# Two-layer streaming encoder in float32 precision: a fused multiply-add for three right operands of layer 1, and four changes of order in the attention part

## The chip, the cores and the metric

The kernel runs on one core of a Trainium2 chip. Its time is the device time of the whole program in microseconds (us), taken as the median over several executions. The engines of the core are TensorE (PE, matrix products), VectorE (DVE), ScalarE (ACT), GpSimd (POOL) and SyncE (SP), on whose queue all transfers between device memory and the on-chip SBUF are issued. Each engine works its instructions off in order and waits on semaphores for the others. Matrix products land in PSUM banks, from which an instruction of DVE or ACT takes them (an eviction).

## The reference

The input `x` has 2048 rows of 1024 floats. Layer 1 is a gated mixer, layer 2 a banded attention; both add to the residual stream, and a norm ends the whole:

```python
h = rms_norm(x, a_norm_g)
u, v, z = split(h @ w_in, 3)              # 1024 x 6144
v = layer_norm(gelu(v), ln_g, ln_b)
y = gelu(u) * (w_s_masked @ v + b_s) * silu(z)   # in groups of 128 rows
x = x + y @ w_out                          # 2048 x 1024
k, v = split(rms_norm(x, g_kv) @ w_kv, 2)
q, z = split(rms_norm(x, b_norm_g) @ w_qz, 2)
o = softmax(q k^T / 8 + rel_bias, over 9 chunks of 64) v     # 16 heads of 64
x = x + (o * silu(z)) @ wb_out
return rms_norm(x, final_norm_g)
```

## The kernel before

**Precision.** Every float32 operand is split into a high part `hi` (rounded to the matmul's format) and the remainder `lo`; a product is three matmuls, `hi*hi`, `hi*lo` and `lo*hi` (lines 118 to 120, so that one product is told by three lines). The split is an ACT copy and a DVE subtraction (line 446).

**Layer 1.** `h @ w_in` is cut into six column blocks `n = 0..5` (two for v, four for u and z), and `y @ w_out` is block `"o"`. Each block is a 2x2-block Strassen-Winograd product: seven products ("phases" 1 to 7, in the order 1, 2, 6, 5, 7, 4, 3) of a left operand S, made of row blocks of x, and a right operand T, made of the weights' quarters `rw_<phase>_<row><column><q>`. A phase has eight steps j, one 512-column product P of twelve matmuls each, in one of four PSUM banks (tag "mm"). `evict` (line 600 and about) adds P into the tiles x, y, c and d, with the row factor `rs` of the norm on some of them.

The norm's gain `ga` belongs to the weights' rows. Before the change, `make_t` applied it so: in phases 1, 2 and 3 together with the split (`fused`: ACT writes `hi = w*ga`, DVE `lo = w*ga - hi` in one scalar_tensor_tensor, line 527); in phases 7, 4 and 6 by ACT multiplications in place (line 494, for block 0 of phase 6 by DVE, line 492), after which POOL made the Winograd sums (`comb`, line 454), half by half: phase 6 `t1 = b12 - b11`, kept in a tile `ch`, then `b22 - t1*ga`; phase 7 `b22 - b12`; phase 4 `b21 - (the result of phase 6)`. Phase 5 takes `t1*ga` as it is and splits it whole (1024 columns).

**What sets the order.** Layer 1's work is laid out by steps: `add_t` puts the load, the sum (`combine`) and the split (`finish`) of each right operand at offsets in steps before the phase that uses it (`offs`); `at` and `put` do this for the scaling of x (`x_scale`), the layer norm of v (`va`, `vl`, lines 878 to 888), the mixing and the stores. The tile scheduler then orders each engine's instructions; dependencies without a semaphore (`behind`, `in_order`, `on_beat`, `paced_by_pj`) pin one instruction behind another on an engine. The raw weights of a block have four buffers ("raw"), so each later load waits until an earlier one has been used up.

In block 0, x itself is scaled by its row factors while the products run: `x_scale(blk, half)` multiplies half of a row block (`ha`, `hb`) by the factors `rbc` (line 794), the first half at step j + 3, the second at j + 22.

**Attention.** It goes over four stretches t of 512 rows and, in each, over eight pairs p of heads. A pair has eight units u (two heads by four blocks of 128 rows): scores s (line 1495), softmax (lines 1503 to 1514, the last being POOL's scaling of `pr`), transposes tp (1530), their split into pt (1534, 1535), and `value`, the product pv (1555), drained by `drain` (1574, 1575) through a tile `ot`. Into the gaps between them `ahead` feeds other matmuls by `take`: the projections pj of the next pair's q, k and z (`project` and `gate`, weights `raw_b`, line 253) and the output projection of the previous stretch (`outs`), `SHARE[t][p]` steps of it per pair. The last stretch's own output products come after its last pair; their left operand's sums are made in `last_open` and `last_sums` on POOL, before and between the units of the last pair. The first q of a pair are copied from one half of the partitions to the other by a transfer (line 1425) before a score can use them.

Of the kernel before, what the change touches and what calls it, by code (L numbers as in the profile page):

```python
# [9 lines left out]
F32 = mybir.dt.float32  # L10
# [23 lines left out]
def trunk_kernel(  # L34
# [57 lines left out]
    ga = cst.tile([P, KD], F32, name="ga")  # L92
    kg = cst.tile([P, KD, 1], F32, name="kg")
# [152 lines left out]
    def weights(t, p, c):  # L246
        name = f"b{t}_{p}_{c}"
        raw = raw_w(t, f"raw_{name}")
        w = w_tile(f"wh_{name}"), w_tile(f"wl_{name}")
        if t or p < 2:  # L250
            nc.sync.dma_start(raw[:], wk3[p][c][:])
        else:
            nc.sync.dma_start(raw[:], w_kqz[p, :, c, :])
# [138 lines left out]
    with ExitStack() as actx:  # L392
# [64 lines left out]
        def make_t(n, ph, src, nq, where, chain_of):  # L457
# [10 lines left out]
            fused = n != "o" and ph in (1, 2, 3)  # L468
# [14 lines left out]
            def combine(q):  # L483
# [3 lines left out]
                def gain(t, r, dve=False):  # L487
                    for i in range(2) if n != "o" and not fused else ():
                        t_ = t[:, i * 512 : i * 512 + 512]
                        k = r * 4 + q * 2 + i  # L490
                        if dve:
                            nc.vector.tensor_scalar(t_, t_, ga[:, k : k + 1], None, op0=mul)
                        else:
                            nc.scalar.mul(t_, t_, ga[:, k : k + 1])
                    return t

# [5 lines left out]
                elif ph == 7:  # L502
                    v = raw(1, 1)
                    comb(v, v, raw(0, 1))
                elif ph == 4:
                    v = chain[n](q)
                    comb(v, raw(1, 0), v)
                elif ph == 5:
                    v = chain[n](2 + q)
                else:  # L510
                    if q == 0:
                        chain[n] = chain_of()
                    b22 = raw(1, 1)
                    t1 = comb(chain[n](2 + q), rows.pop((0, 1, q)), rows.pop((0, 0, q)))
                    v = comb(chain[n](q), b22, gain(t1, 0, n == 0))
                vs[q] = v

            def finish(q):
                out[q] = where(q)
                if fused:  # L520
                    for i in range(2):
                        c_ = slice(i * 512, i * 512 + 512)
                        k = need[0][0] * 4 + 2 * q + i
# [267 lines left out]
        def x_scale(blk, half):  # L791
            h = (hb if blk % 2 else ha)[blk // 2]
            h_ = h[:, half * 512 : half * 512 + 512].rearrange("p (k c) -> p k c", k=4)
            nc.vector.tensor_tensor(
                h_, h_, rbc[:, blk].broadcast_to([P, 4, P]), op=mul
            )

# [175 lines left out]
        for n in range(6):  # L973
            for ph in PH:
                where = in_t(n, ph)
                s = start.get((n, ph), start[0, ph])
                if n == 0 or (n == 1 and ph in (1, 2)):
                    offs = ((-6, 1), (-5, 1), (-3 if (n, ph) == (0, 6) else -4, 1))
# [16 lines left out]
        at(-LOOK, lambda: (x_load(0), nc.sync.dma_start(ga[:], a_norm_g)))  # L995
# [3 lines left out]
        for j in range(NJ):  # L999
# [8 lines left out]
            put(j + 22, x_scale, 2 * j, 1)  # L1008
# [367 lines left out]
    with ExitStack() as bctx:  # L1376
# [103 lines left out]
        def score(t, p, u):  # L1480
# [33 lines left out]
            nc.gpsimd.tensor_scalar(  # L1514
                pr[:, c0:], pr[:, c0:], sl, 1.0, op0=ALU.mult, op1=ALU.mult
            )
# [50 lines left out]
        def drain(t, p, hd, po):  # L1567
# [5 lines left out]
            ot = sb.tile([P, T], F32, tag="ot", name=f"ot{t}_{h}", bufs=1)  # L1573
# [79 lines left out]
        def last_open():  # L1653
# [10 lines left out]
            def third():  # L1664
                for cs in (slice(0, 512), slice(512, 1024)):
                    on_beat(tg(la["s3"][:, cs], la["00"][:, cs], la["10"][:, cs], op=sub))
# [7 lines left out]
        def last_sums(cs):  # L1674
            x_ = {n: a[:, cs] for n, a in la.items()}
            return [
                lambda a=a, b=b, c=c, op=op: on_beat(tg(x_[a], x_[b], x_[c], op=op))
# [233 lines left out]
        def o_all(t):  # L1911
# [4 lines left out]
            (0,) * 8, (0, 0, 0, 0, 13, 13, 22, 8), (7, 7, 7, 7, 7, 7, 14, 0), (6, 6, 6, 6, 6, 7, 7, 12)  # L1916
# [66 lines left out]
        for u in range(2):  # L1983
            take(first, 4)
# [109 lines left out]
```

## Time and profile before

| | us |
|---|---|
| median of three runs (lowest, highest) | 2630.78 (2628.39, 2632.53) |
| profiled execution | 2632.79 |
| its span | 2631.0 |
| PE busy in it | 2582.2 |
| DVE, ACT, POOL busy | 1926.8, 1412.9, 904.4 |

The span runs from the first to the last instruction of the profiled execution. An engine's busy time leaves out waiting. A view by stretches gives each engine's busy time between two moments of the span, the clock that TensorE was granted (1.00 is full) and the share of the time in which the transfer engines were busy. A view of waits gives for each instruction group how long it stood idle and what ended that.

### The profile page before, as it was taken

The page shows a single profiled execution, that of the slowest core. Times are in us where ns is not written, and L with a number is a line of the kernel's source. Part 1 is how long each engine was busy: PE and PEld are TensorE (multiplying, and loading weights), DVE is VectorE, ACT ScalarE, POOL GpSimd, SP SyncE. Part 2 cuts the span into 40 slices and gives each one's busy share as a digit, 9 for nine tenths or more (in the row PEclk, how much of TensorE's full clock was granted, in tenths as well). Part 3 has the DMA queues.
Part 4 walks back from the last instruction along what each step waited for, and adds up shares of the span by engine and source line. Part 5 has one row for each costly group of instructions (what it writes and reads, how often), then busy time and mean ns, then how long its engine had stood idle before and what let it go on. Part 6 is the DMA issues. An engine that isn't in the chain of part 4 may idle for free.

```text
span 2631.0 us, 37991 instructions
## 1 busy us (share of the span) xinstructions
PE 2582.2 (98%) x12752; PEld 2156.3 (82%) x12752; DVE 1926.8 (73%) x3050; ACT 1412.9 (54%) x2521; POOL 904.4 (34%) x875
## 2 busy tenths in 40 slices
PE   9999999999999999999999999999999999999997
PEld 7788788888888888888788878888887888888886
DVE  5984796876768667767857767778777777877677
ACT  7553373553544535443345556666656655666564
POOL 3812245163251323204134234344342322332245
PEclk9999999999999999999999999999999999999999
DMA  8899978989899879878887677778787666775666
GB/s 314 288 351 341 363 278 320 344 303 358 316 338 328 304 262 330 318 243 297 293 305 252 204 237 231 231 247 266 237 277 260 220 208 221 250 228 163 193 226 253
DMA packets 281346, 723.46 MB, mean 275 GB/s; under 512 B 29760, under 2 KB 69696, under 8 KB 281152
## 3 DMA queue, kind: packets, MB, share of 16 engines
q1 hardware_dynamic: 281152, 721.03, 78.8%
q8 instruction: 102, 1.67, 0.3%
q14 instruction: 92, 0.75, 0.1%
HBM read 528.50 MB, written 181.93 MB: 270 GB/s over the span
## 4 chain that ended last, share of the span: by engine, by line
PE 81%; DMA 6%; DVE 6%; ACT 2%; issue 2%; POOL 1%; SPq 0%; DVEq 0%; POOLq 0%; ACTq 0%
PE P L118 9%; PE P L120 9%; PE P L119 9%; PE pj L118 6%; PE pj L120 6%; PE pj L119 6%; PE pv L1555 5%; PE s L1495 4%; PE tp L1530 4%; PE Po L120 4%; PE Po L119 4%; PE Po L118 4%; PE vp L120 2%; PE vp L119 2%; PE vp L118 2%
## 5 line engine op out<-in xcount | busy, mean ns | idle before, releaser
L118 PE MATMUL P<-T,S 128*128 128x512 f32 x1248 | 494.8, 396 | 13.7 <-DVE x L602 5.1
L120 PE MATMUL P<-T,S 128*128 128x512 f32 x1248 | 488.3, 391 | 0.0
L119 PE MATMUL P<-T,S 128*128 128x512 f32 x1248 | 487.9, 391 | 0.3 <-DVE T L527 0.3
L1514 POOL TENSOR_SCALAR pr<-pr,ns 128x640 f32<-128x640 f32 (+4 forms) x256 | 208.6, 815 | 529.6 <-DVE ns L1513 448.4
L118 PE MATMUL pj<-hh_b,wh_b 128*128 128x512 f32 x768 | 319.4, 416 | 0.2 <-ACT wh_b L235 0.2
L120 PE MATMUL pj<-hh_b,wl_b 128*128 128x512 f32 x768 | 303.9, 396 | 0.9 <-DVE wl_b L236 0.9
L119 PE MATMUL pj<-hl_b,wh_b 128*128 128x512 f32 x768 | 302.8, 394 | 0.1
L1510 ACT ACTIVATE pr<-pr,ns 128x640 f32<-128x640 f32 (+4 forms) x256 | 195.5, 764 | 191.9 <-DVE ns L1503 191.0
L118 PEld LDWEIGHTS P<-T,S 128*128 128x128 f32 x1248 | 235.2, 188 | 63.3 <-DVE x L602 3.6
L120 PEld LDWEIGHTS P<-T,S 128*128 128x128 f32 x1248 | 235.0, 188 | 50.9 <-DVE S L446 0.4
L119 PEld LDWEIGHTS P<-T,S 128*128 128x128 f32 x1248 | 235.4, 189 | 45.3 <-DVE T L527 0.6
L1535 DVE TENSOR_TENSOR pt<-tp,pt 128x640 fp32r<-128x640 f32 (+4 forms) x256 | 188.4, 736 | 44.5 <-ACT pt L1534 41.8
L1503 DVE CUSTOM_DVE_ANT_0 pr<-s,bias 128x640 f32<-128x640 f32 (+4 forms) x256 | 188.0, 734 | 36.5 <-PE s L1495 30.8
L1534 ACT CAST pt<-tp 128x640 fp32r<-128x640 f32 (+4 forms) x256 | 158.9, 621 | 52.9 <-PE tp L1530 48.1
L1530 PE MATMUL tp<-ident,pr 128*128 128x128 f32 x1120 | 166.6, 275 | 10.9 <-DVE pt L1535 10.2
L120 PEld LDWEIGHTS pj<-hh_b,wl_b 128*128 128x128 f32 x768 | 144.5, 188 | 35.2 <-DVE wl_b L236 2.9
L1530 PEld LDWEIGHTS tp<-ident,pr 128*128 128x128 f32 x1120 | 130.4, 141 | 46.6 <-issue 16.9
L118 PEld LDWEIGHTS pj<-hh_b,wh_b 128*128 128x128 f32 x768 | 145.3, 189 | 18.2 <-ACT wh_b L235 1.9
L119 PEld LDWEIGHTS pj<-hl_b,wh_b 128*128 128x128 f32 x768 | 145.5, 189 | 16.8 <-DVE hl_b L193 0.6
L1555 PEld LDWEIGHTS pv<-pt,V 128*128 128x128 f32 x896 | 143.2, 188 | 18.5 <-DVE pt L1535 2.6
L1555 PE MATMUL pv<-pt,V 128*128 128x256 f32 (+3 forms) x896 | 153.8, 319 | 0.4 <-DVE pt L1535 0.4
L236 DVE TENSOR_TENSOR wl_b<-raw_b,wh_b 128x1024 fp32r<-128x1024 f32 x96 | 120.7, 1259 | 25.9 <-ACT wh_b L235 25.0
(308 smaller groups left out, 5852.0 us busy)
## 6 DMA issues: line engine op xcount, KB each, us to landing
S<-hsd SPq DMA_DIRECT2D x224, 512.0 KB, 5.9
rw<-in_w_a SPq DMA_DIRECT2D x108, 512.0 KB, 6.4
raw_b<-wk SPq DMA_DIRECT2D x78, 512.0 KB, 4.2
A<-ytd SPq DMA_DIRECT2D x72, 512.0 KB, 6.3
hsd<-S SPq DMA_DIRECT2D x56, 512.0 KB, 5.8
V<-vhd SPq DMA_DIRECT2D x56, 512.0 KB, 5.5
bias<-reld SPq DMA_DIRECT2D x64, 320.0 KB, 4.0
va<-vd SPq DMA_DIRECT2D x32, 512.0 KB, 5.9
```

What stands on the lines that cost most here:

```text
L118: first = mm(ps, lh, rh, start=first, stop=False)
L119: mm(ps, lh, rl, start=False, stop=False)
L120: mm(ps, ll, rh, start=False, stop=last)
L236: tv(wl[:], raw[:], wh[:].bitcast(F32), op=sub)
L1495: mm(ps[:, sg, :w], q[:, qb * P : (qb + 1) * P], kx[:, koff + sg * w : koff + (sg + 1) * w], start=i == 0, stop=i == 1,)
L1503: nc.vector.tensor_tensor_reduce(out=pr[:, c0:].rearrange("p (a b) -> p a b", a=nseg), in0=ps[:, :nseg, :w], in1=bias[:, c0:].rearrange("p ...
L1510: nc.scalar.activation(pr[:, c0:], pr[:, c0:], AF.Exp, scale=-1.0, bias=nm, accum_out=sl)
L1514: nc.gpsimd.tensor_scalar(pr[:, c0:], pr[:, c0:], sl, 1.0, op0=ALU.mult, op1=ALU.mult)
L1530: ins = tpose(tp[:, b, :], pr[:, b * P : (b + 1) * P], ident[:])
L1534: nc.scalar.copy(oh, tp[:, b0:5, :].rearrange("p a b -> p (a b)"))
L1535: nc.vector.tensor_tensor(pt[:, 2560 + o + b0 * P : 2560 + o + 640], tp[:, b0:5, :].rearrange("p a b -> p (a b)"), oh.bitcast(F32), op=ALU ...
L1555: mm(po[:, q0 * P : q1 * P], vtl[t, p][:, i, hs], rhs, start=(i == blocks[0] and j == 0), stop=(i == 7 and j == 1),)
```

## The change

It has these parts.

1. Right operands of phases 6, 7 and 4 of all six blocks: no ACT gain on the weights that are subtracted, and no POOL subtraction. DVE does both in one `scalar_tensor_tensor` per half (`times`): `b22 + t1*(-ga)`, `b22 + b12*(-ga)`, `b21*ga - v`. The gain of `b22` remains on ACT. POOL keeps `t1 = b12 - b11`. A constant `nga = -ga` is made once. Phase 5 joins the fused phases: its gain and split go together, half by half.
2. Block 0: phase 6's loads, sums and splits stand at steps -7, -6 and -3 (before: -6, -5, -3); the second half of an even block's `x_scale` moves from j + 22 to j + 32 and is pinned behind the latest eviction.
3. Attention, start: the load of the raw weights of pair 3, part 1, is ordered behind the projection matmul eight places back (`paced_by_pj(ins, 8)`), and the first `take` before the first score is 6 then 2, instead of 4 and 4.
4. Attention, end: `SHARE` of the last stretch; POOL's sums of the last pair (`third`, `last_sums`) are pinned behind the latest softmax scaling (`on_ease`) instead of, or besides, the latest transposes.
5. The drain tile `ot` is taken from the tag "C" with its four buffers (shared with the output stage's tiles) instead of a tag of its own with one.

How the first part moves the work: on DVE, phase 2 of block 0. Before (ch is the tile of phase 6's operand, c the evictions of phase 2, ha and hb row blocks of x, S left operands):

```order
57 L613 SCALAR_TENSOR_TENSOR c_1_945<-P_2_1_932,rs,x_1_526 128x512
62 L492 TENSOR_SCALAR ch_1063<-ch_1063,ga 128x512
64 L446 TENSOR_TENSOR S_2_7_1113<-ha_649,S_2_7_1113 128x512
66 L613 SCALAR_TENSOR_TENSOR c_2_994<-P_2_2_981,rs,x_2_574 128x512
67 L492 TENSOR_SCALAR ch_1063<-ch_1063,ga 128x512 x2
69 L446 TENSOR_TENSOR S_6_0_1173<-ha_389,S_6_0_1173 128x512
70 L613 SCALAR_TENSOR_TENSOR c_3_1037<-P_2_3_1024,rs,x_3_611 128x512
```

and with the change:

```order
55 L511 SCALAR_TENSOR_TENSOR ch_1013<-ch_1013,nga,rw_6_110_956 128x512 x2
57 L639 SCALAR_TENSOR_TENSOR c_1_947<-P_2_1_934,rs,x_1_528 128x512
63 L511 SCALAR_TENSOR_TENSOR ch_1013<-ch_1013,nga,rw_6_111_1011 128x512
64 L639 SCALAR_TENSOR_TENSOR c_2_1002<-P_2_2_989,rs,x_2_576 128x512
65 L511 SCALAR_TENSOR_TENSOR ch_1013<-ch_1013,nga,rw_6_111_1011 128x512
69 L459 TENSOR_TENSOR S_2_7_1119<-ha_651,S_2_7_1119 128x512
70 L639 SCALAR_TENSOR_TENSOR c_3_1052<-P_2_3_1039,rs,x_3_613 128x512
```

The scalings of `ch` on DVE are gone; multiply-adds that take the raw weight as their third operand stand in about the same places, the second pair of them around an eviction of c_2.

On DVE, phase 6 of block 2, where the layer norm of v goes on beside the products (va and vl are its tiles, x the evictions). Before:

```order
386 L602 TENSOR_TENSOR x_1_3210<-P_6_1_3665,x_1_3210 128x512
387 L446 TENSOR_TENSOR vl_1_0_3696<-va_1_0_3569,vh_1_0_3695 128x1024
388 L602 TENSOR_TENSOR x_2_3239<-P_6_2_3699,x_2_3239 128x512
389 L887 SCALAR_TENSOR_TENSOR va_1_3_3795<-va_1_3_3795,lmv,lg_2970 128x512 x2
390 L602 TENSOR_TENSOR x_3_3259<-P_6_3_3718,x_3_3259 128x512
```

With the change:

```order
410 L628 TENSOR_TENSOR x_1_3196<-P_6_1_3647,x_1_3196 128x512
411 L459 TENSOR_TENSOR vl_1_0_3678<-va_1_0_3551,vh_1_0_3677 128x1024
412 L916 SCALAR_TENSOR_TENSOR va_1_2_3698<-va_1_2_3698,lrs,lb_2957 128x512
413 L511 SCALAR_TENSOR_TENSOR rw_7_111_3881<-rw_7_011_3883,nga,rw_7_111_3881 128x512 x2
414 L628 TENSOR_TENSOR x_2_3225<-P_6_2_3681,x_2_3225 128x512
415 L511 SCALAR_TENSOR_TENSOR ch_3328<-rw_4_100_3915,ga,ch_3328 128x512 x2
416 L628 TENSOR_TENSOR x_3_3245<-P_6_3_3700,x_3_3245 128x512
417 L915 SCALAR_TENSOR_TENSOR va_1_3_3781<-va_1_3_3781,lmv,lg_2956 128x512 x2
```

Between the split of `va_1_0`, which frees a buffer, and the first use of `va_1_3`, which is loaded into it, now stand multiply-adds of phases 7 and 4 and the eviction of x_3.

On SP's queue, the start of attention. Before:

```order
1056 L1318 DMA vhd_137<-v_011_13735 128x4x256
1057 L253 DMA raw_b_3_1_14392<-in_w_kqz 128x1024
1058 L1472 DMA bias_0_13757<-reld_158 128x640
1059 L1425 DMA Qh_0_0_13786<-Qh_0_0_13786 64x512
1060 L1425 DMA Ql_0_0_13787<-Ql_0_0_13787 64x512
```

With the change:

```order
1056 L1347 DMA vhd_137<-v_011_13689 128x4x256
1057 L1501 DMA bias_0_13711<-reld_158 128x640
1058 L1454 DMA Qh_0_0_13740<-Qh_0_0_13740 64x512
1059 L1454 DMA Ql_0_0_13741<-Ql_0_0_13741 64x512
1071 L1454 DMA Ql_1_1_13856<-Ql_1_1_13856 64x512
1072 L1501 DMA bias_2_13920<-reld_160 128x640
1073 L255 DMA wk_1_71<-raw_b_2_1_14069 128x1024
1074 L264 DMA raw_b_3_1_14346<-in_w_kqz 128x1024
```

The load of raw_b_3_1 has left its place ahead of the first q copies and stands behind those of the second pair.

The diff, cut to its core:

```diff
+    nga = cst.tile([P, KD], F32, name="nga")
...
+    eased = []
+
+    def on_ease(ins):
+        tc.add_manual_dep(
+            ins.ins, eased[-1],
+            mybir.DependencyInfo(mybir.DependencyClass.NoSync, mybir.DependencyReason.DATA),
+            reason="order",
+        )
+        return ins
...
-            nc.sync.dma_start(raw[:], w_kqz[p, :, c, :])
+            ins = nc.sync.dma_start(raw[:], w_kqz[p, :, c, :])
+            if (p, c) == (3, 1):
+                paced_by_pj(ins, 8)
...
-            fused = n != "o" and ph in (1, 2, 3)
+            fused = n != "o" and ph in (1, 2, 3, 5)
...
+                def times(o, x_, g, r, y_, op):
+                    for i in range(2):
+                        c = slice(i * 512, i * 512 + 512)
+                        k = r * 4 + q * 2 + i
+                        nc.vector.scalar_tensor_tensor(
+                            o[:, c], x_[:, c], g[:, k : k + 1], y_[:, c], op0=mul, op1=op
+                        )
...
                     v = raw(1, 1)
-                    comb(v, v, raw(0, 1))
+                    if n == "o":
+                        comb(v, v, raw(0, 1))
+                    else:
+                        times(v, rows.pop((0, 1, q)), nga, 0, v, add)
                 elif ph == 4:
                     v = chain[n](q)
-                    comb(v, raw(1, 0), v)
+                    if n == "o":
+                        comb(v, raw(1, 0), v)
+                    else:
+                        times(v, rows.pop((1, 0, q)), ga, 1, v, sub)
...
                     b22 = raw(1, 1)
-                    t1 = comb(chain[n](2 + q), rows.pop((0, 1, q)), rows.pop((0, 0, q)))
-                    v = comb(chain[n](q), b22, gain(t1, 0, n == 0))
+                    b12, b11 = rows.pop((0, 1, q)), rows.pop((0, 0, q))
+                    t1 = comb(chain[n](2 + q), b12, b11)
+                    v = chain[n](q)
+                    times(v, t1, nga, 0, b22, add)
...
+            if half and not blk % 2:
+                behind(ins, last["evict"])
...
-                    offs = ((-6, 1), (-5, 1), (-3 if (n, ph) == (0, 6) else -4, 1))
+                    o = 1 if (n, ph) == (0, 6) else 0
+                    offs = ((-6 - o, 1), (-5 - o, 1), (-4 + o, 1))
...
-            put(j + 22, x_scale, 2 * j, 1)
+            put(j + 32, x_scale, 2 * j, 1)
...
-            ot = sb.tile([P, T], F32, tag="ot", name=f"ot{t}_{h}", bufs=1)
+            ot = sb.tile([P, T], F32, tag="C", name=f"ot{t}_{h}", bufs=4)
...
-                    on_beat(tg(la["s3"][:, cs], la["00"][:, cs], la["10"][:, cs], op=sub))
+                    on_ease(tg(la["s3"][:, cs], la["00"][:, cs], la["10"][:, cs], op=sub))
...
-                lambda a=a, b=b, c=c, op=op: on_beat(tg(x_[a], x_[b], x_[c], op=op))
+                lambda a=a, b=b, c=c, op=op: on_ease(on_beat(tg(x_[a], x_[b], x_[c], op=op)))
...
-            (0,) * 8, (0, 0, 0, 0, 13, 13, 22, 8), (7, 7, 7, 7, 7, 7, 14, 0), (6, 6, 6, 6, 6, 7, 7, 12)
+            (0,) * 8, (0, 0, 0, 0, 13, 13, 22, 8), (7, 7, 7, 7, 7, 7, 14, 0), (5, 5, 5, 6, 6, 6, 7, 16)
...
-            take(first, 4)
+            take(first, 6 if u == 0 else 2)
```

More of the change, by code (lines that the diff above doesn't have):

```diff
@@ L485, in combine, with gain @@
                     return
-                def gain(t, r, dve=False):
+                def gain(t, r):
                     for i in range(2) if n != "o" and not fused else ():
@@ L490, in gain @@
                         k = r * 4 + q * 2 + i
[L491 to L494, printed above, removed]
-                    return t
+                        nc.scalar.mul(t_, t_, ga[:, k : k + 1])
+                    return t
+                def times(o, x_, g, r, y_, op):
[5 more added lines that the diff above has]
+                        )
                 def raw(r, c):
@@ L522, in finish @@
                         c_ = slice(i * 512, i * 512 + 512)
-                        k = need[0][0] * 4 + 2 * q + i
+                        k = (need[0][0] if need else 0) * 4 + 2 * q + i
                         g_ = ga[:, k : k + 1]
@@ L793, in x_scale @@
             h_ = h[:, half * 512 : half * 512 + 512].rearrange("p (k c) -> p k c", k=4)
-            nc.vector.tensor_tensor(
+            ins = nc.vector.tensor_tensor(
                 h_, h_, rbc[:, blk].broadcast_to([P, 4, P]), op=mul
             )
+            if half and not blk % 2:
+                behind(ins, last["evict"])
         def block_c(j):
@@ L993, in trunk_kernel @@
                 add_t(ts, s, n, ph, w_a[n], 2, where, chain_in(n, "hl" if n else "hh"), offs)
-        at(-LOOK, lambda: (x_load(0), nc.sync.dma_start(ga[:], a_norm_g)))
+        at(-LOOK, lambda: (x_load(0), nc.sync.dma_start(ga[:], a_norm_g), nc.vector.tensor_scalar(nga[:], ga[:], -1.0, None, op0=mul)))
         def put(s, f_, *args):
@@ L1513, in score @@
             nc.vector.reciprocal(sl, sl)
-            nc.gpsimd.tensor_scalar(
+            eased.append(nc.gpsimd.tensor_scalar(
                 pr[:, c0:], pr[:, c0:], sl, 1.0, op0=ALU.mult, op1=ALU.mult
-            )
+            ).ins.name)
             prs[t, h, qb] = pr
```

## The prediction

> **What bounds the kernel now.** I read the page first, then busy time by stretches, then TensorE's waits, then the engines' timelines around the waits that the change can reach. The page:
>
> ```profile
> span 2631.0 us, 37991 instructions
> ...
> PE 2582.2 (98%) x12752; PEld 2156.3 (82%) x12752; DVE 1926.8 (73%) x3050; ACT 1412.9 (54%) x2521; POOL 904.4 (34%) x875
> ```
>
> TensorE (PE) is the bound; the change leaves its matmuls alone. It can only win PE's idle time (2631.0 − 2582.2 = 48.8 us) and what a slow clock costs; it can lose by new idle time. The stretches in which the change acts, PE busy first, the granted clock third from the end:
>
> ```profile
> core 0: us, PE busy (x) PEld busy (x) DVE busy (x) ACT busy (x) POOL busy (x), PEclk, DMA share, GB/s
> ...
> 75.00:105.00 30.00, 27.02 (x112) 21.44 (x110) 25.89 (x35) 18.19 (x31) 23.62 (x18) 0.94 0.71 240
> 105.00:130.00 25.00, 22.80 (x98) 18.01 (x99) 25.00 (x32) 9.77 (x16) 23.37 (x17) 1.00 0.90 327
> ...
> 150.00:176.00 26.00, 26.00 (x117) 21.52 (x116) 23.66 (x35) 16.03 (x25) 6.00 (x4) 1.00 0.93 355
> 176.00:200.00 24.00, 24.00 (x108) 19.87 (x107) 21.62 (x34) 12.87 (x21) 1.12 (x1) 1.00 0.91 331
> ...
> 300.00:330.00 30.00, 27.95 (x120) 22.31 (x121) 21.77 (x41) 11.49 (x19) 3.42 (x3) 1.00 1.03 388
> ...
> 380.00:408.00 28.00, 25.02 (x114) 20.43 (x113) 22.34 (x24) 14.23 (x24) 21.44 (x14) 0.94 0.74 280
> ...
> 1500.00:1530.00 30.00, 27.95 (x122) 22.32 (x121) 13.82 (x34) 11.59 (x26) 4.58 (x10) 0.94 0.79 233
> ...
> 2550.00:2600.00 50.00, 44.51 (x232) 36.02 (x231) 43.53 (x72) 28.78 (x55) 26.84 (x25) 1.00 0.92 312
> ```
>
> PE idles 2.98, 2.20, 0, 0, 2.05, 2.98, 2.05 and 5.49 us in them (stretch minus busy). Three show a clock of 0.94, which is (1 − 0.94) × 28 or 30 = 1.7 to 1.8 us of full-speed work lost on top. What ends those waits:
>
> ```profile
> PE P L118 <- DVE x L602: 5.1, 5, 2.4
> ...
> PE P L118 <- DMA S<-hsd: 3.3, 4, 1.5
> PE P L118 <- DVE rs L777: 2.8, 1, 2.8
> PE s L1495 <- DMA Qh<-Qh: 1.8, 1, 1.8
> ```
>
> Each is an eviction late on VectorE (DVE), which frees a PSUM bank, or a transfer.
>
> **A, the gap at 86 us.** DVE, POOL and PE there (first number: start; second: duration; in brackets: idle before and who ended it):
>
> ```profile
> 80.63 2.93 DVE L492 TENSOR_SCALAR ch<-ch,ga 128x512 f32<-128x512 f32 x2 [1.19 <-POOL ch L454]
> ...
> 85.67 0.74 DVE L613 SCALAR_TENSOR_TENSOR c<-P,rs,x 128x512 f32<-128x512 f32 x1
> ```
> ```profile
> 79.30 2.54 POOL L454 TENSOR_TENSOR ch<-rw,rw 128x512 f32<-128x512 f32 x2
> ...
> 83.94 2.93 POOL L454 TENSOR_TENSOR ch<-rw,ch 128x512 f32<-128x512 f32 x2
> ```
> ```profile
> 86.46 0.71 PE L118 MATMUL P<-T,S 128*128 128x512 f32 x1 [2.81 <-DVE rs L777]
> ...
> 87.40 0.63 PE L120 MATMUL P<-T,S 128*128 128x512 f32 x1
> 87.82 0.63 PE L118 MATMUL P<-T,S 128*128 128x512 f32 x1
> ...
> 90.45 0.40 PE L119 MATMUL P<-T,S 128*128 128x512 f32 x1
> 90.68 0.40 PE L120 MATMUL P<-T,S 128*128 128x512 f32 x1
> ```
>
> DVE waits 1.19 us for POOL's half of the phase-6 operand, scales it for 2.93 us beside a busy POOL, and only then evicts at 85.67; PE restarts after 2.81 us and then goes at 0.42 us a matmul instead of 0.23. The change drops the DVE scalings and POOL's second subtraction, puts one DVE multiply-add per half in their place, and its rows stand a step earlier (POOL's first subtraction ahead of one more block). I expect the whole gap and its slow clock gone: 2.98 + 1.8 = 4.8, less 0.3 that stays, −4.5; bounds −4.8 and 0.
>
> [...]
>
> **B, 117 to 127 us.** DVE is full (25.00 of 25):
>
> ```profile
> 119.81 1.82 DVE L446 TENSOR_TENSOR S<-ha,S 128x512 fp32r<-128x512 f32 x1
> 121.56 1.27 DVE L794 TENSOR_TENSOR ha<-ha,rbc 128x512 f32<-128x512 f32 x2
> 122.75 0.68 DVE L602 TENSOR_TENSOR x<-P,x 128x512 f32<-128x512 f32 x1
> ...
> 126.88 0.67 DVE L446 TENSOR_TENSOR S<-xq,S 128x512 fp32r<-128x512 f32 x1
> ```
>
> The same split takes 1.82 beside POOL and 0.67 without it, and the second halves of x (L794) stand ahead of evictions. The change moves those eight halves ten steps on and takes POOL's eight subtractions for phases 7 and 4 away (8 × about 1.57), but DVE gets multiply-adds between these evictions. Of 2.20 us idle I take −1.5; bounds −2.2 and 0. The moved halves land in 150 to 200, where DVE was busy 45.28 of 50 us: 8 × 0.64 + two multiply-adds for the next block, 1.5, makes 51.9. That is 1.9 too much, hidden as long as free PSUM banks (a product is 12 matmuls × 0.23 = 2.8 us) cover the delay. I price it +0.5; bounds 0 and +4.5 (a gap like A's with its clock).
>
> **C, 403 us** (layer-1 block n=2, phase 6), DVE and SP's queue:
>
> ```profile
> 393.83 1.69 DVE L446 TENSOR_TENSOR vl<-va,vh 128x1024 fp32r<-128x1024 f32 x1
> ...
> 401.18 1.66 DVE L887 SCALAR_TENSOR_TENSOR va<-va,lmv,lg 128x512 f32<-128x512 f32 x2 [5.07 <-DMA va<-vd]
> 402.77 0.68 DVE L602 TENSOR_TENSOR x<-P,x 128x512 f32<-128x512 f32 x1
> ```
> ```profile
> 395.54 0.32 SPq L878 DMA_DIRECT2D va<-vd  x1
> ```
>
> The load of va_1_3 goes out only when vl_1_0 has freed its buffer; DVE stands 5.07 us with the eviction of x_3 behind it. After the change, the order puts one layer-norm step, four multiply-adds and the evictions of x_2 and x_3 between vl_1_0 and va_1_3: 0.7 + 4 × 0.75 + 2 × 0.68 = 5.1 us of work in the wait, and x_3 is out before it. Gap and clock are 2.98 + 1.7 = 4.7; I take −3.7; bounds −4.7 and 0.
>
> **D, the first q copies** (SP's queue, then PE):
>
> ```profile
> 1511.66 0.35 SPq L253 DMA_DIRECT2D raw_b<-in_w_kqz  x1
> ...
> 1512.59 0.51 SPq L1425 DMA_DIRECT2D Qh<-Qh  x1
> ```
> ```profile
> 1518.17 0.30 PE L1495 MATMUL s<-K,Qh 128*128 128x128 f32 x1 [1.80 <-DMA Qh<-Qh]
> ```
>
> The 512 KB load of raw_b_3_1 goes out 0.93 us ahead of the first copy, with the bias load between them. It now stands behind the copies of the second pair; it is used two pairs on, so nobody waits. Its 0.35 us in SP's queue come free, and six more matmuls (6 × 0.23 = 1.4) run before the first score: 1.8 of 2.05 us, before anything is said of the copies landing sooner. With its clock, 2.05 + 1.8 = 3.9; I take −3.5; bounds −3.9 and −1.0.
>
> **The rest of the multiply-adds.** Prices, by group:
>
> ```profile
> L494 ACT ACTIVATE rw<-rw,ga 128x512 f32<-128x512 f32 x96 | 64.5, 714 | 61.0 <-DMA rw<-in_w_a 60.8
> L454 POOL TENSOR_TENSOR ch<-rw,ch 128x512 f32<-128x512 f32 x48 | 75.2, 1586 | 41.3 <-ACT rw L494 35.4 <-DVE x L602 4.7 <-ACT ch L494 1.2
> L454 POOL TENSOR_TENSOR rw<-rw,rw 128x512 f32<-128x512 f32 x24 | 37.3, 1567 | 114.9 <-ACT rw L494 78.6 <-DMA rw<-in_w_a 22.1 <-DVE x L602 14.2
> L527 DVE SCALAR_TENSOR_TENSOR T<-rw,ga,T 128x512 fp32r<-128x512 f32 x60 | 47.7, 833 | 8.8 <-ACT T L526 8.8
> ```
>
> POOL loses 48 + 24 subtractions, 112.5 us; DVE gains 72 multiply-adds at 0.75 to 0.83, 54 to 60 us, of which the four dropped scalings of A (about 5) come off; phase 5's split turns 12 whole splits into 24 halves, about +2. DVE goes from 73% to some 75%. Neither POOL nor ACT was the bound, so their relief pays only through A, B and C. Where DVE has room its extra work costs nothing; in 300 to 1300, where it stands in front of evictions with some slack, I put +1.0 (bounds −1 and +4).
>
> [...]
>
> In-order waiting is the other cost. The gains were ACT's work, and ACT stood 60.8 us waiting for weights (row L494); now DVE itself waits for a late weight, evictions behind it. Before the change most loads land ahead of DVE's new places; some in blocks n=3 to 5 are close. +1.5; bounds 0 and +10.6 (below).
>
> **H, 300 to 330 us.** TensorE waits for S loads queued behind stores of the combined output weights. One store moves four places up and one load ahead of its neighbours; DMA is full (1.03) either way. −0.5 of 2.05; bounds −2 and 0.
>
> **L, the last pair.** DVE is busy 43.53 of 50 and PE idles 5.49. Four more matmul steps are kept for this pair (4 × 3 × 0.23 = 2.8 us) and POOL's softmax scalings go ahead of its last sums; but the evictions that belong to those steps (about 1.9 us of DVE work) come with them. −1.5; bounds −5 and +2. The drain tile in a shared four-buffer tag: in pairs with output-weight sums an odd head's copy stands behind one split, two units later, while its PSUM bank isn't due for several units. 0.
>
> **Sum.** −4.5 − 1.5 + 0.5 − 3.7 − 3.5 + 1.0 + 1.5 − 0.5 − 1.5 = −12.2 us. The profiled execution took 2632.8 (span 2631.0 and 1.8 around it), so 2620.6 there; the median of the runs shown, 2630.8, is 2.0 lower: 2618.6, say 2619.
>
> **Rivals.**
> 1. *New gaps for old.* DVE, 51.9 us of work in 50, lets TensorE run out of banks between 150 and 200 (+4.5 instead of +0.5) and C's place stays as it was, because a multiply-add waits for its weight there (0 instead of −3.7), with a further 1.5 elsewhere: −12.2 + 4.0 + 3.7 + 1.5 = −3.0, 2628. For: DVE's full rows. Against: POOL's relief shortens what runs beside it.
> 2. *Slower: DVE blocks on late weights.* ACT's longest wait for such a weight was 18.8 us:
>
> ```profile
> ACT rw L494 <- DMA rw<-in_w_a: 60.8, 17, 18.8
> ```
>
>    If DVE met that with an eviction behind it, three free banks cover 3 × 2.8 = 8.4, TensorE stands 10.4 and loses 1.7 of clock: 12.1 each. It decides from 8.4 us on; one such event brings −12.2 − 1.5 + 12.1 = −1.6 (2629), two +10.5 (2641). Against: ACT read the weights earlier in its order than DVE will.
> 3. *The change doesn't cover C and D.* If rw_4's load moves with its buffer so that the multiply-adds are not ready in C's wait, and the copies land so much later that D's clock is still lost: C 0, D −1.8: −12.2 + 3.7 + 1.7 = −6.8, 2624, still faster. For: SP's order around these loads changes too. Against: the filler matmuls of D need no transfer.
>
> **How the numbers follow.** Forecast 0.55, rival 3 0.10, rival 1 0.22, rival 2 0.13. 0.2% is 5.3 us, about what a measurement of this kernel can tell from no change: faster (under 2625.5) 0.65, same 0.22, slower 0.13. The range: the gains at their bounds, without costs, are −4.8 − 2.2 − 4.7 − 3.9 − 2 − 3 = −20.6, 2610; upward it takes in rival 1 and the single event of rival 2 with some more, 2634.
>
> **What would show it.** Right: no idle of 2 us at 86, 403 and 1518 and clocks of 1.00 in those stretches (11.7 us of the gain); waits of P on x near 2 instead of 5.1; POOL's L454 groups gone, DVE near 1980 us. Wrong: a wait of DVE on DMA rw with TensorE waiting on an eviction behind it (rival 2), idle between 150 and 200 (rival 1), more idle than 5.5 in 2550 to 2600 (L).

## The result, and the profile after

The changed kernel took 2617.84 us (median of five runs, 2616.39 to 2621.01), the kernel before, run beside it, 2632.53 (2628.39 to 2635.28): a ratio of 0.9949, 95% interval 0.9939 to 0.996. In the last group of experiments the same pair, run again, gave 0.9935 (0.9922 to 0.9947). The profiled execution took 2617.9 with a span of 2616.1, against 2632.8 and 2631.0: 14.9 us less.

The page:

```profile
span 2616.1 us, 37882 instructions
...
PE 2581.1 (99%) x12752; PEld 2157.6 (82%) x12752; DVE 1955.5 (75%) x3131; ACT 1375.3 (53%) x2465; POOL 784.7 (30%) x803
```

TensorE's idle time fell from 48.8 to 35.0 us (span minus busy), its busy time by 1.1. POOL lost 120 us and ACT 38, and DVE gained 29: the gain is not in these sums but in a few stretches. The same ones as in the prediction:

```profile
core 0: us, PE busy (x) PEld busy (x) DVE busy (x) ACT busy (x) POOL busy (x), PEclk, DMA share, GB/s
75.00:105.00 30.00, 30.00 (x135) 24.60 (x134) 27.38 (x39) 17.88 (x32) 16.14 (x12) 1.00 0.91 312
105.00:130.00 25.00, 24.89 (x110) 20.28 (x110) 23.16 (x34) 9.18 (x15) 4.21 (x3) 1.00 0.98 364
150.00:176.00 26.00, 25.57 (x114) 20.74 (x113) 25.20 (x38) 13.27 (x22) 11.67 (x9) 1.00 0.90 324
200.00:330.00 130.00, 126.17 (x546) 102.89 (x545) 85.15 (x137) 38.42 (x59) 13.54 (x11) 0.99 0.95 345
380.00:408.00 28.00, 27.02 (x132) 22.34 (x131) 27.76 (x32) 8.70 (x17) 14.04 (x8) 1.00 0.82 292
1500.00:1530.00 30.00, 29.57 (x144) 23.54 (x143) 16.76 (x46) 16.85 (x39) 9.03 (x18) 1.00 0.88 275
2530.00:2600.00 70.00, 65.96 (x329) 53.79 (x327) 60.59 (x96) 40.26 (x78) 48.13 (x41) 1.00 0.84 304
```

Stretch minus PE busy gives idle times of 0, 0.11, 0.43, 3.83, 0.98, 0.43 and 4.04 us. The three clocks of 0.94 are 1.00 now. Stretch 200 to 330, at 0.99, has a new place below full clock (from 296.26 on, matmuls of 0.63 us instead of 0.39). What ends the waits now (in all, times, longest):

```profile
PE tp L1559 <- DVE pt L1564: 5.9, 11, 0.9
PE P L119 <- DVE vst L728: 2.8, 1, 2.8
PE Po L121 <- DVE So L459: 2.5, 1, 2.5
PE ty L950 <- ACT yo L952: 2.3, 1, 2.3
...
PE P L119 <- DVE x L628: 0.5, 1, 0.5
```

The waits of P on an eviction of x, 5.1 us before, are 0.5; the one on `rs` (gap A) and the one on Qh (D) are off the list. Below the scattered short waits of the transposes (tp) stand three single ones of over 2 us: at 295 us (labelled vst), at 1251 (So) and at 503 (yo). Two of them are old waits: counted in TensorE's order, the same matmuls waited 1.53 us at 300 (for a load of S) and 2.15 us at 1256 (for So) before the change. Only the one at 503 is new.

In DVE's timeline, the place of C:

```profile
386.42 4.08 DVE L511 SCALAR_TENSOR_TENSOR rw<-rw,nga,rw 128x512 f32<-128x512 f32 x2
390.42 0.68 DVE L628 TENSOR_TENSOR x<-P,x 128x512 f32<-128x512 f32 x1
391.02 2.88 DVE L511 SCALAR_TENSOR_TENSOR ch<-rw,ga,ch 128x512 f32<-128x512 f32 x2
393.82 0.68 DVE L628 TENSOR_TENSOR x<-P,x 128x512 f32<-128x512 f32 x1
394.42 2.88 DVE L915 SCALAR_TENSOR_TENSOR va<-va,lmv,lg 128x512 f32<-128x512 f32 x2
```

No row has a bracket, that is, no wait: the 5.07 us in which DVE stood for va are filled with multiply-adds, and x is evicted between them. The place of D, on SP's queue and on TensorE:

```profile
1504.97 0.91 SPq L1454 DMA_DIRECT2D Qh<-Qh  x1
```
```profile
1511.73 0.22 PE L1524 MATMUL s<-K,Qh 128*128 128x128 f32 x1
```

The first copy goes out 6.8 us ahead of the score that uses it (before: 5.6, with a wait of 1.80 in it), and the score waits for nothing.

What the multiply-adds cost on DVE, and the first of the layer norm's two steps, which the change doesn't touch. By group (busy us, mean ns, then the idle time ahead), after:

```profile
L915 DVE SCALAR_TENSOR_TENSOR va<-va,lmv,lg 128x512 f32<-128x512 f32 x64 | 52.2, 836 | 10.1 <-DMA va<-vd 7.4 <-DMA lg<-in_ln_g 2.7
...
L511 DVE SCALAR_TENSOR_TENSOR rw<-rw,nga,rw 128x512 f32<-128x512 f32 x24 | 21.5, 918 | 2.6 <-DMA rw<-in_w_a 2.6
L511 DVE SCALAR_TENSOR_TENSOR ch<-rw,ga,ch 128x512 f32<-128x512 f32 x24 | 21.2, 916 | 5.4 <-DMA rw<-in_w_a 5.4
L511 DVE SCALAR_TENSOR_TENSOR ch<-ch,nga,rw 128x512 f32<-128x512 f32 x24 | 18.9, 813 | 12.4 <-ACT rw L504 11.2 <-issue 1.1
```

and before:

```profile
L887 DVE SCALAR_TENSOR_TENSOR va<-va,lmv,lg 128x512 f32<-128x512 f32 x64 | 62.0, 983 | 16.7 <-DMA va<-vd 16.4 <-DMA lg<-in_ln_g 0.2
```

The 72 multiply-adds took 21.5 + 21.2 + 18.9 = 61.6 us. The same 64 layer-norm steps took 9.8 us less, 0.84 instead of 0.98 us each, and the norm's second step, 64 times too, another 9.2 (60.9 to 51.7). These 19.0 us are most of why DVE grew by 29 us and not by 57 (61.6 less the 4.7 of the four scalings that went). With the sums of before put back (sums_back, below) the two steps took 124.1 us again, against 122.9 before and 103.9 after. So it is the sums that shorten them; that it is by POOL's lighter work beside them fits, but no run tries that alone.

### The profile page after: what moved, and what is told of

Same layout as the page of the kernel before. It is cut to its first block, busy times and chain, and to the rows that moved or that the text cites. A ratio compares the mean times of both kernels' runs of the same rounds, so it can differ in the third digit from the quotient of the medians.

```text
span 2616.1 us, 37882 instructions
## 1 busy us (share of the span) xinstructions
PE 2581.1 (99%) x12752; PEld 2157.6 (82%) x12752; DVE 1955.5 (75%) x3131; ACT 1375.3 (53%) x2465; POOL 784.7 (30%) x803
## 4 chain that ended last, share of the span: by engine, by line
PE 71%; DVE 6%; DMA 5%; issue 2%; ACT 1%; POOL 1%; SPq 0%; DVEq 0%; POOLq 0%; ACTq 0%
PE P L119 7%; PE P L121 7%; PE P L120 7%; PE pj L121 6%; PE pj L119 6%; PE pj L120 6%; PE pv L1584 5%; PE s L1524 4%; PE tp L1559 4%; PE Po L121 3%; PE Po L120 3%; PE Po L119 3%; PE vp L120 2%; PE vp L121 2%; PE vp L119 2%
```

## The experiments

The theory: the gain is the end of single stalls (A, B, C, D) and of the slow clock behind three of them; part is given back where TensorE, now earlier, waits for a chain of transfers. Rivals: relief of POOL as such pays; the moves of order alone pay; the new stalls come from DVE blocking on late weights. Ratios are to the kernel before on the same chip, with 95% intervals.

**sums_back.** The changed kernel with the sums of before (make_t, the steps of block 0's phase 6, no `nga`); all other parts stay.

```diff
-                    o = 1 if (n, ph) == (0, 6) else 0
-                    offs = ((-6 - o, 1), (-5 - o, 1), (-4 + o, 1))
+                    offs = ((-6, 1), (-5, 1), (-3 if (n, ph) == (0, 6) else -4, 1))
...
-                    times(v, t1, nga, 0, b22, add)
+                    v = comb(chain[n](q), b22, gain(t1, 0, n == 0))
```

> The changed kernel with the right operands of phases 6, 7, 4 and 5 as before (ACT gains, POOL subtractions, whole split of phase 5, old steps of phase 6 in block 0); the other changes stay. Theory, the gain is a sum of separate stalls and the fused sums remove those at 86 and 403 us: both gaps of over 2 us come back with their slow clocks (+4.8 and +3.7), while the two gaps that are new with the change, at 295 and 503 us, go back to what they were before (about -2.5 and -3): some 2621 us. Rival, POOL's relief does nearly everything: about 2630. Second rival, the moved x scaling and not the sums took the gap at 86 away: no gap there, about 2615.

Measured: 2630.99 us, 0.9979 (0.9968 to 0.999). A and C in its stretches and on TensorE:

```profile
75.00:105.00 30.00, 25.90 (x113) 20.43 (x113) 24.39 (x33) 17.63 (x31) 23.48 (x19) 1.00 0.70 240
...
330.00:410.00 80.00, 77.83 (x366) 64.92 (x365) 71.81 (x78) 52.64 (x88) 47.35 (x27) 0.98 0.72 272
```
```profile
85.40 0.50 PE L119 MATMUL P<-T,S 128*128 128x512 f32 x1 [2.31 <-DVE rs L790]
...
400.81 0.50 PE L119 MATMUL P<-T,S 128*128 128x512 f32 x1 [2.17 <-DVE x L615]
```

Both gaps are back, of 2.31 and 2.17 us (the first stretch idles 4.1 in all, with two short waits more). C's slow clock is back (0.98 in its stretch, a matmul of 0.62 us at 401.86), A's is not: its stretch stands at 1.00. B is not back: 105 to 200 idles 1.46. There remain waits of 1.1 and 2.2 us about 504 to 509, so that gap doesn't hang on the multiply-adds. The time misses the expected 2621 and lies nearer to the rival's 2630, but sums_alone, next, speaks against that rival. The other rival, that the moves of order alone pay, gets its due: they give this 0.9979, less than half of the gain. This kernel undoes the multiply-adds and block 0's earlier steps of phase 6 together, so for A the two aren't parted; for C, in block 2, only the sums differ.

**sums_alone.** The kernel before with the sums, `nga` and the steps of block 0's phase 6 of the change, and nothing else of it (the reverse of the diff above, applied to the kernel before).

> The kernel before with the fused sums alone (phases 6, 7, 4, 5 and the earlier steps of phase 6 in block 0). Theory: gaps at 86 and 403 us gone (-4.8, -3.7), two gaps of 2 to 3 us with slow clock new near 300 and 510 (+2.5, +3), those at 120 smaller by at most 2, the one at 1518 as before: 2627 to 2631 us. Rival, POOL's relief does nearly everything: 2620 or less.

Measured: 2634.26 us, 0.9992 (0.9983 to 1.0). A and C are gone here too, and POOL is as relieved as after the change (105 to 200: 19.38 us busy); yet nothing measurable is won. Its stretches say why:

```profile
75.00:105.00 30.00, 30.00 (x134) 24.52 (x134) 26.15 (x39) 18.04 (x31) 15.09 (x12) 1.00 0.87 294
105.00:200.00 95.00, 89.59 (x381) 71.87 (x381) 84.18 (x125) 39.79 (x65) 19.38 (x14) 0.98 0.88 325
```

From 105 to 200 TensorE idles 5.4 us at a clock of 0.98, against 2.2 before. What A gave is lost again right behind it, in block 0; the expectation had these gaps smaller. What C gave is lost at yo and So, with waits of 2.78 us at 508 and 3.11 at 1257, each in a stretch below full clock (0.98 from 410 to 520, 0.94 from 1240 to 1300). POOL's relief alone therefore isn't the cause of the gain; as a part of it, beside the moved x, it isn't ruled out.

**xscale_back.** The changed kernel with the second halves of x back at j + 22 and unpinned.

```diff
-            if half and not blk % 2:
-                behind(ins, last["evict"])
...
-            put(j + 32, x_scale, 2 * j, 1)
+            put(j + 22, x_scale, 2 * j, 1)
```

> The changed kernel with the second halves of x's scaling back at step j + 22 and unpinned. Theory: the waits of TensorE on evictions between 105 and 135 us come back (about 2 us in three gaps), no gap at 86, the 0.4 us between 150 and 176 gone or replaced: ratio to the kernel before about 0.0007 nearer to 1 than the changed kernel's 0.9949. Rival, with POOL's subtractions gone VectorE has room there: no gaps over 0.3 us between 105 and 135, ratio unchanged.

Measured: 2627.05 us, 0.9967 (0.9956 to 0.9978). The stretch, and what ended TensorE's waits in it:

```profile
105.00:200.00 95.00, 87.15 (x371) 69.72 (x370) 81.87 (x121) 38.52 (x63) 19.07 (x13) 0.98 0.86 316
```
```profile
PE P L119 <- DVE y L628: 2.5, 1, 2.5
PE P L119 <- DVE x L628: 2.5, 3, 1.3
PE P L119 <- DVE x L660: 1.4, 1, 1.4
```

It idles 7.85 us where the changed kernel idles 0.54 (0.11 in 105 to 130, 0.43 in 150 to 176, nothing in the rest). All three rows, 6.4 of the 7.85 us, are waits for evictions by DVE (a fourth, of 1.2, is for one by ACT). The expectation had the place right but only about 2 us of it. The move of x, step and pin together, which was priced at a loss of 0.5 us, is what lets the sums pay: with the sums in place it is worth 7.3 us of idle time.

**q_load_back and take_back.** D has two edits; each kernel undoes one.

```diff
-            if (p, c) == (3, 1):
-                paced_by_pj(ins, 8)
```

> The changed kernel with the load of raw_b_3_1 back ahead of the first q copies; the six matmuls before the first score stay. In the changed kernel the first copy landed 2.15 us before the first score used it, and 1.36 us of that are the two extra products. Theory, either of the two edits is enough: the copies go out 0.4 us later and take some 0.9 longer behind 512 KB, no gap at the first score, clock 1.00 from 1500 to 1530. Rival, the load is the cause: a gap of 0.7 us or more comes back.

```diff
-            take(first, 6 if u == 0 else 2)
+            take(first, 4)
```

> The changed kernel with four matmul steps before each of the first two scores, as before; the load of raw_b_3_1 stays behind the copies. Theory, either edit is enough: the first copy lands 0.8 us before the score, no gap, clock 1.00. Rival, the six matmuls carry the gain: a gap of 0.7 us or more at the first score, with a slow clock if it passes 2.

One run each, so only the place counts: 2623.29 and 2617.54 us beside a before of 2636.06. TensorE's first scores, with the load back in front, and with the old filler:

```profile
1512.30 0.30 PE L1522 MATMUL s<-K,Qh 128*128 128x128 f32 x1
...
1512.86 0.33 PE L1522 MATMUL s<-K,Ql 128*128 128x128 f32 x1 [0.26 <-DMA Ql<-Ql]
```
```profile
1507.03 0.22 PE L1524 MATMUL s<-K,Qh 128*128 128x128 f32 x1
```

Neither has the gap. The kernel sums_alone, which has neither edit, has it still:

```profile
1500.00:1530.00 30.00, 27.76 (x121) 22.13 (x120) 13.78 (x34) 11.41 (x25) 4.50 (x9) 0.94 0.78 231
```

Either edit alone covers the wait, with a margin close to nothing in the first (Ql is 0.26 late). The prediction gave most of D to the filler; the load's move would have done as well.

**load_late.** The gap at 295 us. Its label names DVE:

```profile
295.13 0.47 PE L119 MATMUL P<-T,S 128*128 128x512 f32 x1 [2.81 <-DVE vst L728]
```

vst, which no matmul reads, ended at 294.98; the left operand's load landed at 294.99. In the repeat of the changed kernel (after_again, below) the wait of the same matmul is put down to the load itself:

```profile
295.60 0.47 PE L119 MATMUL P<-T,S 128*128 128x512 f32 x1 [3.00 <-DMA S<-hsd]
```

On SP's queue that load stood behind a weight load that waited for its buffer:

```profile
280.16 0.65 SPq L582 DMA_DIRECT2D wod<-rwo  x1
285.74 0.33 SPq L493 DMA_DIRECT2D rw<-in_w_a  x1
...
288.49 1.26 SPq L673 DMA_DIRECT2D S<-hsd  x1
```

The experiment puts the loads of the weights of block 1's phase 3 two steps later, and their split one step.

```diff
+                if (n, ph) == (1, 3):
+                    offs = ((-6, 1), (-5, 1), (-4, 1))
```

> The changed kernel with the loads, sums and splits of block 1's phase 3 right operand two, one and one steps later, so that the load of S_4_6 stands ahead of that of rw_3_111 on the queue. Theory: the gap of 2.81 us at 295 is S_4_6's transfer, issued late because the queue stood for rw_3_111's buffer: it shrinks under 1 us, the clock stays at 1.00, about 2614 us. Rival, the gap is what the wait's label says, VectorE late with an eviction behind the splits of T_3: it stays within 0.5 us unless the splits move too, and the time stays at 2617 to 2619.

Measured: 2619.34 us, 0.9931 (0.9918 to 0.9944). The stretch, and TensorE further on:

```profile
200.00:330.00 130.00, 128.68 (x565) 105.40 (x564) 90.29 (x147) 42.38 (x67) 15.49 (x12) 1.00 0.98 359
```
```profile
499.62 1.12 PE L950 MATMUL ty<-ident,y 128*128 128x128 f32 x4 [3.16 <-ACT yo L952]
...
1248.39 0.50 PE L121 MATMUL Po<-To_hh,So 128*128 128x512 f32 x1 [3.10 <-DVE So L459]
1248.72 0.39 PE L119 MATMUL Po<-To_hh,So 128*128 128x512 f32 x1
```

The gap at 295 is gone: the stretch idles 1.32 instead of 3.83 us, at full clock. On SP's queue the load of S now stands ahead of the weights'. DVE's split of these weights moved by a step too, so the run alone doesn't part load and split; the label in the repeat speaks for the load. The waits at 500 and 1248 are longer than in the first profile (3.16 and 3.10 us, with a second of 1.18, against 2.28 and 2.49), but in the repeat, where the gap at 295 stands, they are 2.87 and 3.09: nothing shows that they took over its time. The expected 2614 was not reached. The intervals are some 3 us to either side, about what the gap is worth, so whether its end shortens the kernel stays open.

**both_later.** load_late with, besides, phase 6's loads of block 3 one step later, aimed at the chain behind the gap at 503. There SP's queue stood for 8.5 us, to 497.8, at a weight load, and a store of yo behind it went out only then. The load waited for a buffer that POOL's sum (to 497.75) freed, and that sum had waited 10.0 us for its weight.

```diff
-                    o = -13 if ph == 6 else -5
+                    o = (-12 if n == 3 else -13) if ph == 6 else -5
```

> As load_late, and the loads of phase 6 of block 3 one step later, so that phase 2's second load no longer stands in front of the stores of the transposed y on the queue. Theory: the gap of 2.28 us at 503 is the third copy of a transpose waiting for the store of the first, which stood behind that load: it goes with its slow clock, another 3 to 4 us, about 2610. Rival: the later loads of phase 6 make its sums late and stop TensorE before phase 6, or the queue stands at another load: 2614 to 2618.

Measured: 2618.38 us, 0.9929 (0.9916 to 0.9941). The wait on yo is gone from 499; one of 1.53 us on DVE takes its place, 3.06 us remain at 1248. The expected 2610 was not reached, and again the total can't be told from the changed kernel's: two stalls are smaller, and a gain of their size is at the limit of what these intervals can tell.

**plain_split.** The gap at 1250 lies in block "o", where DVE has the splits of To and So and those of a later product's weights (vs). The theory was that these splits, three in a row, stand ahead of So; the third was moved one step on, on top of both_later.

```diff
-                for ph, rc in ((1, (0, 0)), (2, (1, 0)), (3, (1, 1))):
+                for ph, rc in ((1, (0, 0)), (2, (1, 0))):
                     keep(ph, w[rc])
...
+            def third():
+                keep(3, w[1, 1])
```

> As both_later, and in the preparation of v's weights the third split stands one step after the second instead of right behind it; both go through one buffer, so that VectorE stood 2.5 us for the second's store, with left operands of the output block behind it. Theory: the gap of 2.5 to 3.1 us near 1250 shrinks under 1 us, 2 to 4 us faster than both_later, ratio to before about 0.9918. Rival, what is won is given back where TensorE next meets a chain that it doesn't set (transfers near 1340, the last pair): ratio 0.993.

Measured: 2620.15 us, 0.9942 (0.9929 to 0.9956). The gap stayed, at 3.67 us. DVE and TensorE there:

```profile
1241.31 1.66 DVE L1231 TENSOR_TENSOR vs_3l<-wv,vs_3h 128x512 fp32r<-128x512 f32 x1 [3.56 <-ACT vs_3h L1230]
1242.90 4.53 DVE L459 TENSOR_TENSOR To<-rwo,To 128x1024 fp32r<-128x1024 f32 x2
```
```profile
1249.15 0.79 PE L121 MATMUL Po<-To_hh,So 128*128 128x512 f32 x1 [3.67 <-DVE So L459]
```

The theory of that place falls: with the split moved, DVE waits 3.56 us for ACT in its stead, then the two splits of To take 4.53 us ahead of So. What sets the gap at 1250 stays open.

**end_back, ease_back and ot_back.** The end of attention. end_back undoes the last stretch's `SHARE` row and the pinning of POOL's sums; ease_back the pinning alone; ot_back the drain tile's tag.

```diff
-  (5, 5, 5, 6, 6, 6, 7, 16)
+  (6, 6, 6, 6, 6, 7, 7, 12)
-                    on_ease(tg(la["s3"][:, cs], la["00"][:, cs], la["10"][:, cs], op=sub))
+                    on_beat(tg(la["s3"][:, cs], la["00"][:, cs], la["10"][:, cs], op=sub))
-                lambda a=a, b=b, c=c, op=op: on_ease(on_beat(tg(x_[a], x_[b], x_[c], op=op)))
+                lambda a=a, b=b, c=c, op=op: on_beat(tg(x_[a], x_[b], x_[c], op=op))
```

> The changed kernel with the old shares of the last stretch (6 6 6 6 6 7 7 12) and POOL's last sums pinned as before. Theory: TensorE's idle time in the last pair (50 us from about 12 us after the pair's first score) goes from 2.4 back to 5.5 us, ratio about 0.0012 nearer to 1. Rival, the idle time only moves between pairs, or it came from the drain tile: 2 to 3 us stay, ratio unchanged.

> The changed kernel with POOL's last sums pinned as before; the shares (5 5 5 6 6 6 7 16) stay. Theory, the shares carry the gain at the end: idle time from 2530 to 2600 within 0.7 us of after_again's 4, ratio within 0.0004. Rival, POOL's softmax scalings were late behind the sums: 1.5 us or more of it comes back.

```diff
-            ot = sb.tile([P, T], F32, tag="C", name=f"ot{t}_{h}", bufs=4)
+            ot = sb.tile([P, T], F32, tag="ot", name=f"ot{t}_{h}", bufs=1)
```

> The changed kernel with the drain tile in its own tag with one buffer. Theory, the tag is worth nothing: ratio within 0.0004 of after_again's, idle time from 1530 to 2530 within 1 us of it. Rival, the tag frees ScalarE or delays it: the idle time there changes by 2 us or more (it fell from 8.5 to 5.0 with the change).

Measured: end_back 2622.21 us, 0.9953 (0.9936 to 0.9969); ease_back 2621.97, 0.9943 (0.993 to 0.9955); ot_back 2618.72, 0.9935 (0.9923 to 0.9947).

In the stretch from 2530 to 2600 us end_back idles 5.20 us, ease_back 5.02 and the changed kernel, as it ran beside ease_back, 4.00. That proves little: ot_back and take_back, which keep the new end, idle 5.80 and 5.53 there, and since the kernels reach 2530 us at different moments, the stretch holds different work in each. From 1530 to 2530 the same holds: 8.5 us idle before, 5.0 after, 8.3 in end_back, but 8.0 in both_later, with the new row.

A count of matmuls gives the same work. TensorE runs 12752 in every kernel; numbered by their start, their order differs at the end only between numbers 11140 and 12640, by the `SHARE` row. From the one to the other, before, end_back and sums_alone, with the old row, take 281.4, 281.5 and 282.5 us. The eleven profiled kernels with the new row take 277.1 to 279.8, the changed kernel 277.5 and ease_back 279.1. So the row is worth some 3 us; the pinning can't be told from nothing. The times alone could not have told it: end_back's interval reaches from 0.9936 to 0.9969. No effect of the tag was measured.

**after_again.** The changed kernel once more, beside the last group.

> The changed kernel once more, as the base of this chip for the other three. Both theories: ratio 0.994 to 0.996; gaps of over 2 us near 295, 503 and 1250, since they have a cause in the order and not in one execution; if one is missing here, it was chance.

Measured: 2619.84 us, 0.9935 (0.9922 to 0.9947). The waits at 295 (3.00 us), 503 (2.87) and 1252 (3.09) stand there again: they belong to the program, not to one execution. Their sizes don't: over the seven profiled kernels that are the same up to attention, the one at 295 took 1.51 to 3.09 us. No version of the experiments is measurably faster than this one.

## Why the prediction was right

The forecast was 2619, the time 2617.84; in the profiled execution −12.2 was forecast and −14.9 came. The stages by the same matmuls (change against before, in us; the last column is the repeat):

| matmuls | terms | forecast | change | repeat |
|---|---|---|---|---|
| to 560 | A, B | −6.0 | −7.3 | −6.8 |
| 560 to 860 | moved halves of x | +0.5 | +0.7 | +0.2 |
| 860 to 1300 | H | −0.5 | +3.0 | +3.6 |
| 1300 to 2200 | C | −3.7 | −4.2 | −5.5 |
| 2200 to 5800 | other multiply-adds, late weights | +2.5 | +3.0 | +4.7 |
| 5800 to 7000 | D | −3.5 | −5.5 | −4.2 |
| 7000 to 11140 | none | 0 | −0.7 | −1.2 |
| 11140 to end | L | −1.5 | −4.0 | −3.8 |

The stalls A, B, C and D went as forecast and make the gain. That the total came so near is partly luck: H missed by 3.5 us to one side, L and D by 4.5 to the other. The steps, by stretches:

- **A** (−4.5): 2.98 us idle and 1.8 of clock are gone: −4.8. sums_back brings the gap back, without its slow clock. That the new sums with their earlier steps end the gap is shown; which of the two does it is not.
- **B and the moved halves of x** (−1.5 + 0.5): idle −2.1 and +0.43, so the sum of the two is near. As a step it was mis-sized: the move was taken as a small cost of the change, while sums_alone and xscale_back show that without it 105 to 200 idles 5.4 and 7.85 us. One reading under it was wrong: the split of 0.67 us at 126.88 was not "without" POOL, which is busy for all of 126.88 to 127.55; its subtraction there starts 0.04 us behind the split, while at 119.81 it starts 0.01 ahead. So this pair of rows doesn't show what POOL's absence brings. The parts don't add: the sums alone gave 0.9992, the rest alone 0.9979, all of it 0.9949 and 0.9935 (intervals above).
- **C** (−3.7): 2.98 idle became 0.98, and 1.7 of clock came back: −3.7. sums_back brings gap and clock back, and sums_alone is free of both: shown. The work in the wait, priced at 5.1 us, took 8.7 (385.76 to 394.42), since the multiply-adds took 2.0 and 1.4 us each beside POOL and not 0.75; x was out in time all the same.
- **D** (−3.5): 2.05 became 0.43, with the clock: −3.4. By the same matmuls, 6900 to 7000, it took 25.1 us before, 25.2 in sums_alone and 20.7 after. Each edit is enough by itself, and without both the stall stays.
- **H** (−0.5): the wrong sign, and the step that failed. "One store moves four places up and one load ahead of its neighbours" was true, but it left out that a weight load waits there for its buffer with a load of S behind it. The wait of one and the same matmul for that load grew from 1.53 to 2.81 us, and eight matmuls at about 0.43 instead of 0.23 us from start to start came in addition. By the same matmuls (860 to 1300) the stage took 101.5 us before, 104.6 after, and 99.8 to 100.4 in the three kernels with load_late's edit.
- **The rest of the multiply-adds and DVE's late weights** (+1.0 + 1.5): about the right size, by another mechanism. Between 408 and 1300 TensorE's idle time rose by only 0.2 (by 2.8 in the repeat), and two new slow places, at 505 and 1252, with matmuls of 0.63 us instead of 0.39, cost some 1.4 and 1.6 us, an estimate from the starts of these matmuls. They follow the waits on yo and So, not a multiply-add. Those waits stand in sums_back too, without the multiply-adds; why the one on yo came with the change isn't shown. DVE did stand for late weights, or for ACT's gain on one, 2.6 + 5.4 + 11.2 = 19.2 us in all, once for longer than the 8.4 us at which rival 2 was to decide:

```profile
864.04 1.41 DVE L511 SCALAR_TENSOR_TENSOR ch<-ch,nga,rw 128x512 f32<-128x512 f32 x2 [9.10 <-ACT rw L504]
```
```profile
840.00:880.00 40.00, 40.00 (x198) 33.47 (x197) 27.33 (x39) 23.28 (x39) 4.26 (x3) 1.00 0.93 328
```

  TensorE was busy for all of 40 us around it. In that phase ACT makes the evictions (its line 633 goes on meanwhile), and no eviction stood behind DVE. Rival 2 needs a late weight in a phase whose evictions are DVE's; none came to pass.
- **L** (−1.5): 4.0 by the same matmuls, of which the `SHARE` row is some 3. The direction and the edit were right, the size too small.
- **The clock.** Three slow places went, at 87, 404 and 1521, and three came, at 297, 505 and 1252 (matmuls of 0.63 us instead of 0.39 at all six). Of the 5.3 us that the forecast had for the clock (1.8, 1.7 and 1.8 in A, C and D) nothing is left in the total; the whole gain is idle time, 13.8 us where the forecast had 6.9, and 1.1 us of busy time. Rival 1 (new gaps for old) had a point, but not at the places it named: 150 to 200 idles 0.43, C is gone, and of the three gaps that stand now one is new and one longer than it was.
- **Slips in the working.** Rival 2's whole chance of 0.13 went to "slower", though its single event gives 2629; and the range takes 3 for L, whose bound was 5. Neither moves the forecast.

## What to carry to other kernels

When TensorE is busy for 98% of the time, an edit is worth what it does to single stalls; find them by stretches. A slow clock behind a stall is a price that may or may not be due: here the same stall, at 503, came with it at 2.28 us and without it at 2.87. An edit that moves work onto a full engine needs its companion that moves other work out of the way, and the two must be tried together: here the sums alone brought nothing measurable, and without the moved x the whole change brought about half. Compare two kernels by the same work, by number of matmul, and not by the same microseconds, once one runs ahead of the other; and take a repeat of the kernel before calling a stall new or longer.

## What the runs showed of the hardware

- **The clock and the length of a gap.** In the changed kernel the gap of 2.49 us at 1251 was followed by a slow clock:

```profile
1250.95 0.50 PE L121 MATMUL Po<-To_hh,So 128*128 128x512 f32 x1 [2.49 <-DVE So L459]
...
1253.07 0.63 PE L121 MATMUL Po<-To_hh,So 128*128 128x512 f32 x1
```

  The matmuls there took 0.63 us, 0.43 from start to start; from 1255.63 on they took 0.39 and 0.23. In load_late a longer one at that place, 3.10 us, was not followed by one: the matmul behind it took 0.39 (its rows stand with that experiment). At 503 a wait of 2.28 us was followed by matmuls of 0.63 us (0.98 from 410 to 520), and 2.87 us in the repeat of the same kernel by matmuls of 0.39 and 0.40 (1.00). At 296 in ease_back 1.89 us came with a stretch at 0.99 (200 to 330), and A's 2.31 us in sums_back with matmuls of 0.39 and 0.40 (1.00). In the kernel before, 1.80 us at 1518, with 0.25 more behind it, were followed by matmuls of 0.63 us, and 2.15 at 1256 by matmuls of 0.39 and 0.40; so the 2 us that take_back's rival names for a slow clock were the author's estimate, and these two rows speak against it. Between 1.8 and 3.1 us, then, the length alone doesn't decide; what does is not shown.
- **The label of a wait.** A wait for several semaphores at 295 was put down to DVE, whose instruction ended 0.01 us before a load landed. No matmul reads what the named instruction writes. The repeat puts the same wait down to the load, and with the weights' loads and split moved it was gone.
- **A multiply-add beside POOL.** Two at 386 us, with POOL at work, took 4.08 together; two single ones at 399 and 400 us, with POOL idle, 0.74 each; over all 72 the mean of the groups is 0.81 to 0.92 us. POOL at the first place:

```profile
385.90 2.36 POOL L231 TENSOR_TENSOR wk<-wk,kg 128x1024 f32<-128x1024 f32 x1 [19.31 <-DMA wk<-in_w_kqz]
388.21 8.54 POOL L945 TENSOR_TENSOR c<-c,m 128x512 f32<-128x512 f32 x5
```
